# Side steps ordered with a slack behind their modelled ready time, and output-gate columns one head later, in a one-core hybrid decoder step

## The chip, the cores and the metric

The kernel runs on one core of one Trainium2 chip. The metric is the device time of one execution in microseconds (us), the median of several runs. The engines are TensorE (PE; its weight loads are listed apart as PEld), VectorE (DVE), ScalarE (ACT), GpSimd (POOL) and SyncE (SP), which here issues the DMAs. Each engine works through its own instructions strictly in the order in which the program lists them, and waits on semaphores for the operands that other engines make.

## The reference, cut to what matters

One layer is computed for 1024 prompt tokens and for 64 sample tokens (8 sequences of 8) with the same weights:

```python
proj = einsum("bld,de->ble", x, w_in)
glu_a, glu_b, conv_gate, qkv, dn_gate, beta_in, decay_in, mem_q, mem_gate = split(proj)
u = glu_a * sigmoid(glu_b);  hc, _ = causal_dwconv(u, conv_prev, conv_w)          # width 31
out_conv = silu(layer_norm(hc + conv_b)) * silu(conv_gate)
q, k, v = split(silu(causal_dwconv(qkv, qkv_prev, qkv_conv_w)))                    # width 4
o, s = gated_delta_rule(l2norm(q), l2norm(k), v, g, beta, s0)                       # 8 heads of 128
out_dn = rmsnorm(o) * delta_norm_w * silu(dn_gate)
out_mem = softmax(mem_q @ mem_k.T) @ mem_v * silu(mem_gate)                         # 4 heads, 256 memory tokens
y = layer_norm(alpha * x + concat(out_conv, out_dn, out_mem) @ w_out)
```

All data are float32. The gated delta rule is done in chunks of 128 tokens: for each head a triangular matrix is inverted, and then a chain of four chunks carries a 128x128 state. The states are outputs as well.

## The kernel before, in words

**The large products.** The input projection has 52 blocks of 128 output columns. They are computed in two passes, pass one (p = 0) with 512 prompt and the 64 sample tokens, pass two (p = 1) with the other 512 prompt tokens. `gemm` (one call per block) accumulates 16 slices of the contraction in PSUM, in four quarters of four slices. Every product is made of three matmuls on operands split into a high and a low float32r part (`mm3`): ACT casts the weights (`wh`), DVE or POOL makes the rest (`wl`), in `split_quarter`. In pass one a quarter holds two groups of 12 matmuls on 288 columns; in pass two it holds 12 matmuls on 512 columns. Two products for the memory keys and values (`run_mem`) stand ahead of block 44 of pass one. After both passes comes the output projection (PSUM tiles `om`) with the final LayerNorm.

**The side work.** What follows a block is done beside the later blocks. `finish` takes a finished block out of PSUM and adds Python generators to a list, `side.q`: `gen_conv4` (short convolution), `gen_k` (norm, decay matrices, the triangular inverse), `gen_q`, `gen_v`, `gen_s` (the sample tokens), `gen_chain` (the four chunks, the norm, the output gate), for the other groups `gen_cgroup` and `gen_cln` (wide convolution and its LayerNorm) and `gen_att` (memory attention). A generator issues the instructions of one step, and then yields the tiles that its next step reads. A matmul of a later step thus lands in TensorE's single stream between the matmuls of the large products, and TensorE stands still if its operand isn't there yet.

**The order, and the rough clock.** `Side.tick` decides which steps go in. It is called twice a quarter (in pass one after each group of 12 matmuls, in pass two after six matmuls and again after six more). It goes through the list and takes the next step of each generator whose yielded tiles are "ready" by a rough clock, up to six steps and 1000 ns of TensorE work. The clock is the class `Model`: each engine has a time, each tile a ready time; `Proxy` adds for each instruction a cost by formula while the program is being written. For n elements a partition: float32r matmul n/2.4 + 3 ns, float32 matmul max(n/0.6, 110), transpose 109 (n over 64), DVE 65 + n/0.96, ACT 100 + 0.83 n, POOL 100 + 2 n (tensor-tensor); a tile is ready 170 ns after its instruction ends. A generator that yields nothing goes on at the next tick; one that yields "R" may be continued up to three times a tick without a look at the clock (the 31 x 2 small DVE steps of the inverse, the 31 taps of the wide convolution); "B" means blocked on a Python condition. Nothing of this runs on the chip: the clock fixes the order of the instructions when the program is built.

**The order of the blocks.** `ct_order` lists them. Before, each of the eight heads has K, Q, V and its output gate (`COL_DGATE`), then come the GLU pairs, the convolution gates, the memory queries and the memory gates. So head h has its K block at place 4h. The gate block ends in ACT writing a tile `sgate`, from the pool "W" of 19 buffers that all wide side tiles share; it is read by the last multiplication of `gen_chain` (tile `m`), whose result goes to DRAM (`mx`, and `mxs` for the sample tokens) in `put_mixed`.

**Where the order forces a wait.** When the K block of a new head is finished, `finish` calls `side.drain` if three heads are in flight (`inflight`). A drain calls `tick` again and again, with no matmul of the large products in between, and moves the rough TensorE clock on by 200 ns where nothing was taken, until the oldest head has issued its `mx` DMA. `run_mem` and the start of the output projection drain too, until PSUM banks are free, and `open_out` (12 slices into the output projection) drains until no side work is left.

Nearly every instruction bears line 86 in the profile, that of the helper that records it, so groups are told apart by their tiles.

Of the kernel before, what the change touches and what calls it, by code (L numbers as in the profile page):

```python
# [18 lines left out]
NH = 8  # L19
# [2 lines left out]
LN_EPS = 1e-5  # L22
NORM_EPS = 1e-6
HOLD = 10
NSPLIT = 4 * 2 * 52 + 32 + 9 * KT
QSCALE = 128 ** -0.5
NTOK = (576, 512)
# [3 lines left out]
COL_Q, COL_K, COL_V, COL_DGATE = 12, 20, 28, 36  # L31
COL_MQ, COL_MGATE = 44, 48

def ct_order():
    order = []
    for h in range(NH):
        order += [COL_K + h, COL_Q + h, COL_V + h, COL_DGATE + h]
    for j in range(4):
        order += [COL_GLU_A + j, COL_GLU_B + j]
    order += [COL_CGATE + j for j in range(4)]  # L40
    order += [COL_MQ + j for j in range(4)]
    order += [COL_MGATE + j for j in range(4)]
    return order
# [73 lines left out]
class Side:  # L117
# [7 lines left out]
    def tick(self, budget=1000, n=6, rounds=3):  # L125
        m = self.m
        done = 0
        t0 = m.clk["PE"]
        for rnd in range(rounds):
            for e in list(self.q):  # L130
                if done >= n or m.clk["PE"] - t0 >= budget:
                    return done
                if rnd and e[1] != "R":
                    continue
                if e[1] != "R" and m.ready(e[1]) > m.clk["PE"]:
                    continue
                try:
                    r = next(e[0])
                except StopIteration:
                    self.q.remove(e)  # L140
                    done += 1
                    continue
                if r == "B":
                    e[1] = ()
                    continue
                e[1] = r if isinstance(r, tuple) or r == "R" else ()
                if r != "R":
                    done += 1
        return done
# [12 lines left out]
def hybrid_step(ctx, tc, I, O):  # L162
# [21 lines left out]
    def nm(s):  # L184
        uid[0] += 1
        return f"{s}{uid[0]}"
# [36 lines left out]
    written = set()  # L223

    order = ct_order()
    def wsrc(ap):
        f = ap.rearrange("p k c -> p (k c)")
# [61 lines left out]
    def split_quarter():  # L289
# [6 lines left out]
        nsplit[0] += 1  # L296
        wpool, tg = (Y["p"], "y") if nsplit[0] > NSPLIT - (HOLD - 4) else (wp, "")
        hi = wpool.tile([P, 512], F32R, tag="wh" + tg, bufs=4 if wpool is wp else HOLD - 4, name=nm("wh"))
        lo = wpool.tile([P, 512], F32R, tag="wl" + tg, bufs=4 if wpool is wp else HOLD - 4, name=nm("wl"))
        act.copy(out=hi, in_=s)  # L300
# [9 lines left out]
    def ensure(n):  # L310
        while len(ready) < n:
            if not split_quarter():
                return
# [1201 lines left out]
    for g in range(2):  # L1515
# [5 lines left out]
        for cb, idx in phases:  # L1521
# [8 lines left out]
            def out3(i, k, wh, wl):  # L1530
                b, (o, rows) = bank[i], tiles[i]
                if rows == 64:
                    pe.matmul(out=b, lhsT=xfull[k][:, 512:640], rhs=wh, start=(k == 0), stop=False)
                    pe.matmul(out=b, lhsT=xfull[k][:, 512:640], rhs=wl, start=False, stop=(k == KT - 1))
                    return
                sl = slice(o, o + rows)
                pe.matmul(out=b, lhsT=xh[k][:, sl], rhs=wh, start=(k == 0), stop=False)
                pe.matmul(out=b, lhsT=xl[k][:, sl], rhs=wh, start=False, stop=False)
                pe.matmul(out=b, lhsT=xh[k][:, sl], rhs=wl, start=False, stop=(k == KT - 1))

            for k in range(KT - HOLD if last else KT):
                ensure(1)
# [10 lines left out]
            if last:  # L1553
                held = []
                for k in range(KT - HOLD, KT):
                    ensure(1)
# [4 lines left out]
                side.drain(lambda: side.q)  # L1561
                for k in range(KT - HOLD, KT):
                    out3(3, k, *held[k - KT + HOLD])
# [92 lines left out]
```

## Time and profile before

| | us |
|---|---|
| Median of 3 runs (lowest, highest) | 2072.53 (2071.78, 2075.76) |
| The profiled execution's own time | 2066.65 |
| Span of its trace, first to last instruction | 2064.9 |
| PE busy | 1979.0 |
| PEld busy | 1715.8 |
| DVE busy | 1428.7 |
| ACT busy | 845.9 |
| POOL busy | 602.6 |

The profiled execution is 5.88 us shorter than the median. Its mean granted TensorE clock was 0.989 of full speed. In the lists of the profile a group is named by the tiles it writes and reads (`ps<-rbuf,Y`: a side matmul that reads `rbuf` and `Y` and writes a PSUM tile `ps`; `m<-xh,wl`: one of the input projection). "Idle before" is the time in which the engine stood still ahead of an instruction, with the instruction of another engine that ended the wait. The ends of matmuls are modelled, and successive matmuls overlap in the list: what TensorE needs for one is read from start to start. Times in the trace are counted from the first instruction. Pass one lasts until about 905 us (with the memory products near 717 to 760), pass two until about 1640 us, the output projection until the end.

### The profile page before, as it was taken

Reading aid. Unit: us, or ns where it says so; the run is one execution under the profiler, and the core shown is the slowest. Engines: PE = TensorE matmul, PEld = TensorE weight load, DVE = VectorE, ACT = ScalarE, POOL = GpSimd, SP = SyncE. Lnnn points to the kernel's source line nnn. Section 1 sums busy time; section 2 is a strip of 40 time slices with the busy share of each in tenths; the row PEclk is TensorE's granted clock in tenths of the full one; section 3 lists DMA queues with packets and bytes.
Section 4 is the critical chain, followed back from the end, with each engine's and each line's share of the span. In section 5 each row is a group of like instructions: output and inputs, shape, how many; then the busy total and the mean of one; then the engine's idle time right before and its main releaser. Section 6 shows DMA issues by size and latency. Waiting matters only on the chain.

```text
span 2064.9 us, 33208 instructions
## 1 busy us (share of the span) xinstructions
PE 1979.0 (96%) x12156; PEld 1715.8 (83%) x12156; DVE 1428.7 (69%) x3190; ACT 845.9 (41%) x2013; POOL 602.6 (29%) x680
## 2 busy tenths in 40 slices
PE   8999999999999989989999999999989999999995
PEld 7999999999999969977777887787767788877784
DVE  6778877887789984245787776779985433348447
ACT  5444444444433335364444444443326522235124
POOL 5434333443323342113333333322322100006003
PEclk9999999999999999999999999999999999999998
DMA  6232233323223255354332223332232463345444
GB/s 205 84 107 83 97 97 102 93 81 105 90 88 107 96 168 171 108 176 149 96 92 90 74 89 103 102 92 82 90 101 92 153 203 106 106 160 181 142 131 144
DMA packets 107267, 239.50 MB, mean 116 GB/s; under 512 B 32224, under 2 KB 36576, under 8 KB 106848
## 3 DMA queue, kind: packets, MB, share of 16 engines
q1 hardware_dynamic: 107104, 237.39, 36.3%
q8 instruction: 95, 1.56, 0.3%
q14 instruction: 68, 0.56, 0.1%
HBM read 210.24 MB, written 27.10 MB: 115 GB/s over the span
## 4 chain that ended last, share of the span: by engine, by line
PE 36%; DVE 13%; issue 2%; ACT 2%; POOL 1%; DMA 1%; SPq 0%; POOLq 0%; DVEq 0%; ACTq 0%
PE om L86 17%; PE m L86 16%; PE ps L86 4%; DVE hc L86 4%; DVE cv L86 2%; DVE wl L86 2%; DVE y L86 1%; DVE xt L86 1%; DVE X L86 1%; DMA raw<-mx 0%; ACT wh L86 0%; ACT L86 0%; POOL wl L86 0%; POOL y L86 0%; DMA mvs<-out_mem_v_dram 0%
## 5 line engine op out<-in xcount | busy, mean ns | idle before, releaser
L86 PE MATMUL m<-xh,wh 128*128 128x288 f32 (+1 forms) x2496 | 859.4, 344 | 3.6 <-ACT wh L86 3.5
L86 PE MATMUL m<-xh,wl 128*128 128x288 f32 (+1 forms) x2496 | 819.8, 328 | 12.3 <-DVE wl L86 9.6
L86 PE MATMUL m<-xl,wh 128*128 128x288 f32 (+1 forms) x2496 | 816.4, 327 | 0.0
L86 ACT CAST wh<-raw 128x512 fp32r<-128x512 f32 x592 | 359.5, 619 | 398.9 <-PE om L86 221.4
L86 POOL TENSOR_TENSOR wl<-raw,wh 128x512 fp32r<-128x512 f32 x221 | 307.3, 1391 | 728.1 <-ACT wh L86 687.1
L86 PEld LDWEIGHTS m<-xh,wl 128*128 128x128 f32 x2496 | 469.3, 188 | 54.3 <-DVE wl L86 15.1
L86 PEld LDWEIGHTS m<-xh,wh 128*128 128x128 f32 x2496 | 470.5, 188 | 47.0 <-issue 11.1
L86 PEld LDWEIGHTS m<-xl,wh 128*128 128x128 f32 x2496 | 470.9, 189 | 30.2 <-issue 2.7
L86 DVE TENSOR_TENSOR wl<-raw,wh 128x512 fp32r<-128x512 f32 x371 | 283.2, 769 | 264.7 <-ACT wh L86 264.1
L86 DVE SCALAR_TENSOR_TENSOR hc<-u,cvc,hc 128x512 f32<-128x512 f32 x360 | 243.8, 721 | 3.1
L86 PE MATMUL om<-wl,xh 128*128 128x512 f32 x576 | 227.8, 395 | 10.3 <-DVE wl L86 9.2
L86 PE MATMUL om<-wh,xh 128*128 128x512 f32 x576 | 227.4, 395 | 3.9 <-ACT wh L86 2.7
L86 PE MATMUL om<-wh,xl 128*128 128x512 f32 x512 | 201.7, 394 | 0.0
L86 DVE TENSOR_TENSOR xt<-mb,X 128x8 f32<-128x8 f32 (+30 forms) x496 | 183.0, 369 | 11.8
L86 DVE SCALAR_TENSOR_TENSOR cv<-xr,qcw,cv 128x512 f32<-128x512 f32 (+1 forms) x216 | 167.1, 774 | 7.7
L86 POOL TENSOR_TENSOR y<-y,lnb 128x512 f32<-128x512 f32 (+1 forms) x32 | 51.7, 1639 | 342.6 <-DVE y L86 222.9
L86 PEld LDWEIGHTS om<-wl,xh 128*128 128x128 f32 x576 | 109.6, 190 | 37.8 <-DVE wl L86 13.7
L86 PEld LDWEIGHTS om<-wh,xh 128*128 128x128 f32 x576 | 109.5, 190 | 28.8 <-ACT wh L86 3.8
L86 ACT ACT_TABLE_LOAD x89 | 114.2, 1283 | 44.4 <-DVE smz L86 25.7
L86 DVE TENSOR_REDUCE X<-xt 128x4 f32<-128x8 f32 (+30 forms) x496 | 110.2, 222 | 10.6
L86 PEld LDWEIGHTS om<-wh,xl 128*128 128x128 f32 x512 | 97.4, 190 | 20.3
L86 ACT ACTIVATE oi<-ps,GT 128x128 f32<-128x128 f32 x56 | 20.6, 368 | 207.4 <-DVE r L86 192.8
(307 smaller groups left out, 2032.0 us busy)
## 6 DMA issues: line engine op xcount, KB each, us to landing
raw<-in_wt_dram SPq DMA_DIRECT2D x208, 512.0 KB, 3.8
raw<-in_wo_dram SPq DMA_DIRECT2D x72, 512.0 KB, 3.9
mb<-ysc SPq DMA_DIRECT2D x128, 64.0 KB, 2.2
raw<-mx SPq DMA_DIRECT2D x16, 512.0 KB, 3.9
xt<-in_xp_dram SPq DMA_DIRECT2D x32, 256.0 KB, 4.4
out_y_p_dram<-y SPq DMA_DIRECT2D x32, 256.0 KB, 2.8
raw<-in_xa_dram SPq DMA_DIRECT2D x16, 288.0 KB, 3.9
S<-in_sdelta_dram SPq DMA_DIRECT2D x16, 256.0 KB, 4.7
```

The source lines that it names most:

```text
L86: r = fn(**kw)
```

## The change

A step that waits for tiles is taken only when the rough TensorE clock has passed the ready time of its tiles by 800 ns or more; steps that yield nothing, "R" or "B" are treated as before. The blocks get a new order: K0 Q0 V0, K1 Q1 V1 gate0, K2 Q2 V2 gate1, ..., K7 Q7 V7 gate6, gate7, then as before. So K of head h (h from 1) stands at place 4h - 1, one place earlier than before, and its gate at place 4h + 6 instead of 4h + 3 (head 7: 31 both times).

```diff
+SLACK = 800
...
     for h in range(NH):
-        order += [COL_K + h, COL_Q + h, COL_V + h, COL_DGATE + h]
+        order += [COL_K + h, COL_Q + h, COL_V + h] + ([COL_DGATE + h - 1] if h else [])
+    order += [COL_DGATE + NH - 1]
...
-                if e[1] != "R" and m.ready(e[1]) > m.clk["PE"]:
+                if e[1] != "R" and e[1] and m.ready(e[1]) + SLACK > m.clk["PE"]:
                     continue
```

## The prediction

> **What bounds the kernel now.** The page comes first: its span and the busy time of the engines.
>
> ```profile
> span 2064.9 us, 33208 instructions
> PE 1979.0 (96%) x12156; PEld 1715.8 (83%) x12156; DVE 1428.7 (69%) x3190; ACT 845.9 (41%) x2013; POOL 602.6 (29%) x680
> ```
>
> TensorE carries the time, and the change takes no matmul away. It can gain only where TensorE stands still: 2064.9 - 1979.0 = 86 us, and a little more inside what counts as busy. The second view is the list of waits on TensorE, longest in total first (us, times, longest).
>
> ```profile
> PE mm L86 <- DVE wl L86: 9.8, 4, 4.2
> PE m L86 <- DVE wl L86: 9.6, 13, 1.7
> PE om L86 <- DVE wl L86: 9.2, 6, 5.3
> PE ps L86 <- DVE rbuf L86: 5.6, 9, 1.2
> ...
> PE ps L86 <- DVE S L86: 3.3, 3, 2.2
> ...
> PE ps L86 <- ACT oms L86: 2.5, 1, 2.5
> PE ps L86 <- DVE ut L86: 2.4, 5, 0.5
> PE ps L86 <- ACT cv L86: 2.2, 2, 1.4
> PE ps L86 <- DVE pt L86: 1.4, 3, 0.9
> ...
> PE ps L86 <- POOL lsum L86: 1.2, 1, 1.2
> PE ps L86 <- DVE cq L86: 0.9, 2, 0.7
> PE ps L86 <- DVE r L86: 0.8, 2, 0.5
> ...
> PE ps L86 <- ACT GT L86: 0.6, 1, 0.6
> PE ps L86 <- DVE Rc L86: 0.5, 1, 0.5
> ```
>
> The first three rows are waits for weights; the change doesn't touch how these are split. The eleven `ps` rows are side matmuls whose operand came late: 21.4 us in 30 waits. This is what a later place in the order can remove. The third view, the timeline of one such wait, shows how it comes about (start, duration, instruction).
>
> ```profile
> 399.76 1.27 DVE L86 TENSOR_SCALAR cv<-xr,qcw 128x64 f32<-128x64 f32 x1
> 400.21 0.29 PE L86 MATMUL m<-xl,wh 128*128 128x288 f32 x1
> 400.34 0.29 PE L86 MATMUL m<-xh,wl 128*128 128x288 f32 x1
> 401.07 1.00 DVE L86 SCALAR_TENSOR_TENSOR cv<-xr,qcw,cv 128x64 f32<-128x64 f32 x3
> 401.54 0.29 PE L86 MATMUL m<-xh,wl 128*128 128x288 f32 x1
> 402.10 0.28 DVE L86 COPY rbuf<-ps 32x128 f32<-32x128 f32 x1
> 402.44 0.67 PE L86 MATMUL ps<-rbuf,Y 64*64 64x64 f32 x8 [0.61 <-DVE rbuf L86]
> ```
>
> The four `cv` operations on 64 elements hold VectorE for 1.27 + 1.00 = 2.27 us, while the rough clock counts 4 x (65 + 64/0.96) = 0.53 us. The copy into `rbuf` stands behind them in VectorE's queue, so its tile is late by more than the clock believes, and TensorE waits. The matmuls start 400.34 - 400.21 = 0.13 us apart though each is listed with 0.29: so a listed wait of 0.61 us is really 402.44 - 401.54 - 0.13 = 0.77 us. The 30 waits thus cost about 21.4 + 30 x 0.16 = 26 us.
>
> That addition can be set against the Trainium skill, "Perfetto Trace Analysis", section "Identifying the Most-Contended Engine": matmul busy time says little about the distance to the limit, since the instructions are pipelined, and the busy share of the weight loads says more. By the page's rule the PEld row (83%) would leave room for well over 26 us; the starts in the timeline support the part of it that is added here, and no row says that side operands cause more.
>
> **The change part by part.** *The 800 ns.* For the `rbuf` step the working by the formulas is this. Three copies of 65 + 128/0.96 = 198 ns follow the matmuls before; with 170 ns of hand-over at either end the tiles are ready 934 ns after them. The next tick comes after 12 matmuls, 12 x 123 = 1476 ns by the same clock, so the step went in at the first tick. With the slack it needs 1734 ns and goes in one tick later, 12 x 0.13 = 1.6 us in the trace. That covers 0.77 us. All eleven rows but `S` (longest 2.2) and `oms` (2.5) have a longest wait below one tick, so if every late step moves by a tick some 24 of the 26 us go. But the margin has to stand against a lag of VectorE that the clock doesn't see, here 2.27 - 0.53 = 1.7 us, and steps that were on time may now stand behind such a group. I keep three quarters, 18 us; the bounds are 8 (a third) and 26, plus 2 for waits too short to be listed, 28.
>
> *What the slack costs.* The matmuls themselves are the same, so TensorE pays nothing directly. The cost is that every head takes longer. From the code, the longest path through a head's generators has 28 steps that wait for tiles. The pace at present, in pass two:
>
> ```profile
> 1093.24 0.39 PE L86 MATMUL ps<-S,cv 128*128 128x128 f32 x2
> 1093.67 0.35 DVE L86 SCALAR_TENSOR_TENSOR r<-ps,GT,vs 128x128 f32<-128x128 f32 x1 [0.36 <-PE ps L86]
> 1094.86 0.38 PE L86 MATMUL ps<-r,ubuf 128*128 128x128 f32 x2
> 1095.28 0.35 DVE L86 TENSOR_SCALAR ut<-ps,kz 128x128 f32<-128x128 f32 x1 [0.49 <-PE ps L86]
> 1096.46 0.27 PE L86 MATMUL ps<-ut,kd 128*128 128x128 f32 x1
> ```
>
> One link of the chain takes one tick, 1094.86 - 1093.24 = 1.62 us. By the clock's formulas such a link is ready 170 + 198 + 170 = 538 ns after its matmuls; with the slack 1338 ns, where a tick in pass two is 6 x 216 = 1296 ns plus whatever other side matmuls fall between. So about half of the links move by a tick; in pass one, with 1476 ns, most don't. A growth of 0.8 x 28 = 22 us for a head in pass two is the middle; the bounds are 5 us (the order of VectorE's queue hides most of it) and 28 x 1.62 = 45 us.
>
> Does anyone wait for a head's end? Only the drain at the K block of the fourth head. In the new order that block stands at place 11, where the gate of the third head stood, so the row of that gate gives its time:
>
> ```profile
> 179.72 0.33 SPq L86 DMA_DIRECT2D mx<-m  x1
> 215.37 0.71 ACT L86 ACTIVATE sgate<-m 128x288 f32<-128x288 f32 x2
> 1076.11 0.38 SPq L86 DMA_DIRECT2D mx<-m  x1
> 1081.25 0.60 ACT L86 ACTIVATE sgate<-m 128x512 f32<-128x512 f32 x1
> 1095.05 0.59 ACT L86 COPY xr<-m 128x512 f32<-128x512 f32 x1
> ```
>
> In pass one head 0 is done at 179.7 and the block comes at 215.4, a margin of 36 us: no drain. In pass two head 0 is done at 1076.1. Before, K of head 3 came at 1095.05, 19 us later; now at 1081.25, 5.1 us later. A growth of 22 us makes a drain of 22 - 5 = 17 us, or 17/1.62 = 10 links. In a drain nothing lies between the links, and one takes from the matmul's start to the end of its VectorE operation, 1095.28 + 0.35 - 1094.86 = 0.8 us, and some 0.1 to go on, so 9 us, of which about 3 are side matmuls (0.38 for each link) that have to be done anyway: 6 us of standstill. Later heads start one place (1095.05 - 1081.25 = 14 us) earlier too and so lose no spacing: K to K of the fourth next head stays 12 places, and head 4 onwards gives back at most its present margin. The bounds are 0 (growth below 5) and (45 - 5)/1.62 x 0.9 = 22 us.
>
> *The gate one head later.* The gate of head h comes seven places after its K, so about 7 x 14 = 98 us in pass two; the chain needs it only at its end. Head 0's K comes first in the pass, and the gate's new place 6 lies well ahead of 1076 less the time of place 11 down to 6 (1081.25 - 5 x 14 = 1011), so no chain waits for it. The gate's buffer of pool "W" is held for three places, some 42 us, less in each head; in exchange other tiles live longer by the slack. I put both at nothing: no list of the engines' waits names a W tile waiting for its buffer, and if the cover goes it shows as late weights.
>
> *The heads against the wide convolution.* Two stretches are bound by VectorE, by the windows view (length, PE, PEld, DVE busy):
>
> ```profile
> 647.00:717.00 70.00, 70.00 (x523) 69.56 (x522) 70.00 (x133) 21.49 (x40) 18.12 (x16) 1.00 0.31 102
> 1470.00:1540.00 70.00, 61.49 (x250) 46.26 (x250) 65.10 (x76) 16.62 (x27) 22.31 (x16) 0.98 0.32 99
> ```
>
> Heads 6 and 7 end just ahead of them, start 14 us earlier and take 22 us longer, so 8 us net of their VectorE work could slide in. As TensorE stands still for 8.5 of 70 us in the second, an eighth of 8 us is 1 us; bounds -3 (they end earlier) and +3. The end of pass two is safe: the last side DMA is issued at 1655.07 and the drain in `open_out` lies 12 slices of the output projection, each 14 matmuls of 0.23 us, behind 1640: at about 1679.
>
> ```profile
> 1655.07 0.43 SPq L86 DMA_DIRECT2D mx<-om  x1
> ```
>
> POOL's part of a step moves with it and nothing of the large products waits behind it but the low parts of the weights, split two quarters ahead. On SP the DMAs of the side steps (`mx`, the inverse's transfers, the states) move back with their steps, past weight loads that stood behind them. A load then waits less for a side tile; as five loads are kept ahead, I count nothing, and if that cover goes it is the `wl` rows that grow.
>
> *The sum.* -18 + 6 + 1 = -11 us. The profiled execution's 2066.65 would become 2055.6. The shown median lies 5.9 us above that execution, and a prediction is compared with medians, so 2072.5 - 11 = 2061.5; I give 2061.
>
> **The rivals.** *Slower: the drain eats more than the waits gave.* Place: K of head 3 in pass two (and of heads 4 to 7 if their margins go too). It decides once the growth of a head is over about 5 + 20 = 25 us in links of 1.6 us; at the full 45 us it costs 22, and the gain at its lower end is 8, so +14; middle +6, 2078. For: the margin of 5.1 us is read straight off two rows. Against: in a drain the links take half their usual time, which limits the price. Whether long standstills also slow the clock shows here:
>
> ```profile
> 739.00:745.00 6.00, 5.38 (x13) 4.22 (x14) 6.00 (x14) 0.85 (x2) 0.00 (x0) 0.50 0.82 257
> ```
>
> In the 6 us around the 4.2 us wait for `wl` the granted clock is 0.50. The links of a drain leave gaps of about 0.5 us, so by this row alone I add nothing. The Trainium skill, "TensorE: Matmul & The Clock Gate", section "HAM oscillation — how this bites in real kernels", puts the limit at gaps of about 3.4 us; the row agrees. By that rule a drain that ends in one long wait, for a DMA of the inverse for instance, would run some microseconds at half speed, which speaks against this change.
>
> *No change: the waits only move.* VectorE's unseen lag is 1.7 us in the timeline above, twice the slack, and 26 us of waits is 30 cases among several hundred side steps; a shifted order could meet as many. Then the gain is about 8 and the drain takes 6 to 10 of it: 2071.
>
> *The change doesn't do what it says:* the steps could have been late by the order of the queues alone, so that a step moved back takes its VectorE work back too. For the operand of a step this is not so (it is issued one step earlier), but the chain as a whole keeps its relations. The time would be as in the rival before; I count it there.
>
> **How the numbers follow.** The forecast, faster by the removed waits less one drain, has a chance of 0.66; no change 0.16; slower 0.18. Runs of the kernel before lie within 0.2% (4 us), about what a measurement can tell from no change. The forecast's own range is 2044 (28 us gained, no drain) to 2068. The whole range reaches up to the slower rival's middle: 2044 to 2078. Faster by over 0.2% gets 0.66, within it 0.16, slower 0.18.
>
> **What would show it.** Right: the `rbuf` row of TensorE's waits falls from 5.6 us to below 1, the `ps` rows together from 21.4 to below 8; the weight rows (`wl`) stay within 3 us of theirs; head 0's `mx` DMA in pass two comes some 10 to 20 us later than 1076, and beside it TensorE has a short stretch of many `ps` steps without `m` matmuls. Wrong: `ps` rows of the same total under other names (the waits moved), several such stretches in pass two, or `wl` rows that have grown (buffers or queues of POOL and ACT held up).

## The result and the profile after

The changed kernel takes 2108.02 us (median of 4 runs, 2106.89 to 2110.30), the kernel before 2072.16 on the same chip (4 runs, 2071.35 to 2075.76). The ratio is 1.0171, with a 95% interval of 1.0153 to 1.0189: 36 us slower, where 11 us faster was forecast. The profiled execution of the changed kernel took 2106.89 us. Its page, engines first:

```profile
span 2105.2 us, 33200 instructions
PE 1992.1 (95%) x12156; PEld 1723.8 (82%) x12156; DVE 1440.8 (68%) x3190; ACT 850.5 (40%) x2015; POOL 609.0 (29%) x680
```

The matmuls are the same 12156. The span grew by 40.3 us, 4.4 more than the medians, since the profiled execution of before lies 5.5 us under its median and this one 1.1. TensorE's busy time grew by 13.1, so its idle time by 27. The list of TensorE's waits (total us, times, longest) answers to the one of before:

```profile
PE ps L88 <- DVE S L88: 19.3, 10, 3.3
PE ps L88 <- DVE ut L88: 14.6, 13, 2.8
PE mm L88 <- DVE wl L88: 10.0, 4, 4.2
PE om L88 <- DVE wl L88: 9.1, 4, 5.2
PE m L88 <- DVE wl L88: 8.4, 12, 2.3
...
PE ps L88 <- DVE r L88: 4.1, 5, 1.3
...
PE ps L88 <- ACT cv L88: 3.7, 5, 1.0
PE ps L88 <- DVE X L88: 3.0, 2, 1.8
```

The three weight rows hold what they held (27.5 us against 28.6). The `rbuf` row is gone, as announced. But `S`, `ut` and `r`, the three tiles that the chain of a head makes one after the other, went from 3.3, 2.4 and 0.8 us to 19.3, 14.6 and 4.1. All `ps` rows together are 51.2 us in 43 waits, where before they were 21.4 in 30. That is 29.8 us more.

The timeline of one of the four longest such waits, in pass two, TensorE's and VectorE's rows with GpSimd's:

```profile
1183.39 0.49 DVE L88 TENSOR_SCALAR cv<-xr,qcw 128x512 f32<-128x512 f32 x1
...
1183.89 1.30 POOL L88 TENSOR_TENSOR Dm<-D,triu 128x512 f32<-128x512 f32 x1
1183.92 4.95 DVE L88 SCALAR_TENSOR_TENSOR cv<-xr,qcw,cv 128x512 f32<-128x512 f32 x3
...
1185.27 1.37 POOL L88 TENSOR_TENSOR D<-D,kzn 128x512 f32<-128x512 f32 x1
...
1186.60 1.71 POOL L88 TENSOR_TENSOR wl<-raw,wh 128x512 fp32r<-128x512 f32 x1
...
1187.06 0.39 PE L88 MATMUL m<-xh,wl 128*128 128x512 f32 x1
...
1188.79 0.26 DVE L88 TENSOR_REDUCE X<-xt 128x4 f32<-128x116 f32 x1
...
1189.08 0.36 DVE L88 TENSOR_TENSOR xt<-mb,X 128x120 f32<-128x120 f32 x1
...
1190.39 0.34 DVE L88 SCALAR_TENSOR_TENSOR S<-S,GT,ps 128x128 f32<-128x128 f32 x1
...
1190.78 0.71 PE L88 MATMUL ps<-S,cv 128*128 128x128 f32 x4 [3.34 <-DVE S L88]
```

TensorE takes a matmul every 0.23 us here, so it stands still from 1187.29 to 1190.78, 3.5 us. The operation that it waits for, on the state `S` of one head, takes 0.34 us; it starts at 1190.39 because VectorE works through its queue in order, and ahead of it lie the convolution of the Q block of the head after next (three `cv` operations, 4.95 us together while GpSimd's `Dm` and `D` and then a `wl` run beside them; nearly alone such three take 2.33 us, and there is a row of that at the end) and then five operations of the inverse of the head between the two, 1188.79 to 1190.39. The rough clock counts 3 x (65 + 512/0.96) = 1.8 us and 5 x 0.19 = 0.95 us for these eight, together 2.75; the trace shows 1190.39 - 1183.92 = 6.47. The 3.7 us between come close to the standstill of 3.5. This chain is that of head 2, behind the Q block of head 4. The same wait, 3.3 us in the list, comes again at 1253, 1315 and 1377, in the chains of heads 3, 4 and 5, behind the Q blocks of heads 5, 6 and 7.

A long wait costs more than its length. Three stretches of 4 us from the windows view, each beginning where a wait ended (of 2.19, 2.84 and 3.34 us); the third number from the right is the granted clock:

```profile
528.99:532.99 4.00, 4.00 (x20) 4.00 (x21) 3.83 (x13) 0.87 (x2) 0.25 (x1) 0.58 0.02 4
179.61:183.61 4.00, 4.00 (x31) 4.00 (x32) 3.86 (x13) 0.00 (x0) 0.25 (x2) 1.00 0.34 131
1190.78:1194.78 4.00, 4.00 (x17) 3.53 (x18) 2.18 (x6) 0.87 (x2) 0.80 (x1) 0.63 0.27 78
```

After the 3.34 us wait the clock is 0.63 for 4 us, which is 4 x 0.37 = 1.5 us lost; so the wait is worth about 5 us, and the four of them 20. Over the span the mean granted clock went from 0.989 to 0.984: time lost at a low clock is 2105.2 x 0.016 = 33.7 us, before 2064.9 x 0.011 = 22.7, and so 11 us more. The listed side waits (+29.8) and the clock (+11) make up the 40 us; the lower clock is where most of the 13 us of busy time came from (behind the wait above, matmuls start 1192.64 - 1192.21 = 0.43 us apart, not 0.23). The Trainium skill, "TensorE: Matmul & The Clock Gate", section "HAM oscillation — how this bites in real kernels", puts the limit at idle gaps above about 3.4 us. The trace agrees for the waits of 3.3 us (3.5 from start to start) and differs below: the clock fell after one of 2.19 us, and not after one of 2.84.

Where in the kernel it is lost, by the start of a block's first matmul in the two timelines (us, after less before): pass one +1 at block 8, +5 at 16, +15 at 24, +20 at 32, +20 at 44; pass two +14 at its start, +21 at 16, +32 at 24, +44 at 32, +38 at 48; the output projection begins 40 us later. It grows only while heads are in flight; a little is given back elsewhere.

### The profile page after: what moved, and what is told of

Read it like the earlier page. It is cut to its first block, busy times and chain, and to the rows that moved or that the text cites. A ratio compares the mean times of both kernels' runs of the same rounds, so it can differ in the third digit from the quotient of the medians.

```text
span 2105.2 us, 33200 instructions
## 1 busy us (share of the span) xinstructions
PE 1992.1 (95%) x12156; PEld 1723.8 (82%) x12156; DVE 1440.8 (68%) x3190; ACT 850.5 (40%) x2015; POOL 609.0 (29%) x680
## 3 DMA queue, kind: packets, MB, share of 16 engines
q8 instruction: 95, 1.56, 0.3%
## 5 line engine op out<-in xcount | busy, mean ns | idle before, releaser
L88 DVE TENSOR_TENSOR wl<-raw,wh 128x512 fp32r<-128x512 f32 x371 | 273.4, 743 | 255.9 <-ACT wh L88 248.9
L88 DVE SCALAR_TENSOR_TENSOR cv<-xr,qcw,cv 128x512 f32<-128x512 f32 (+1 forms) x216 | 189.8, 879 | 7.7
L88 PEld LDWEIGHTS om<-wh,xh 128*128 128x128 f32 x576 | 109.9, 191 | 30.6 <-ACT wh L88 5.5
L88 PEld LDWEIGHTS om<-wh,xl 128*128 128x128 f32 x512 | 98.0, 191 | 20.5
```

What stands on the lines that cost most here:

```text
L88: r = fn(**kw)
```

## The experiments

The theory after the result: *the order meets VectorE's backlog*. A step's place is chosen by a clock that doesn't see how late VectorE runs; shifting steps puts chain links behind other work in VectorE's queue, by several us, against which 0.8 us is nothing. The rivals: *longer heads are the cost themselves* (drains, more tiles alive), *the slack on the chain delays the chain*, *the order of blocks does it*, *GpSimd's products beside VectorE do it*. All runs in one table; "side waits" are the `ps` rows of TensorE's waits in the profiled execution, and the clock is its mean granted one. Each ratio is against runs of the kernel before on the same chip.

| run | median us | ratio (95%) | side waits, us in times | clock |
|---|---|---|---|---|
| before (profile) | 2072.5 | 1 | 21.4 in 30 | 0.989 |
| after | 2108.0 | 1.0171 (1.0153 to 1.0189) | 51.2 in 43 | 0.984 |
| e1 order only | 2083.5 | 1.0055 (1.0034 to 1.0075) | 28.1 in 31 | 0.989 |
| e2 slack 300 | 2100.4 | 1.0133 (1.0116 to 1.0151) | 43.8 in 42 | 0.983 |
| e3 products on VectorE | 2094.2 | 1.0101 (1.0085 to 1.0118) | 30.6 in 31 | 0.982 |
| e4 products later | 2105.7 | 1.0157 (1.0142 to 1.0172) | 45.3 in 30 | 0.981 |
| e5 old order, slack 300 | 2095.1 | 1.0113 (1.0097 to 1.0129) | 40.9 in 48 | 0.987 |
| e6 chain 14 ticks later | 2124.9 | 1.0259 (1.0245 to 1.0273) | 57.5 in 36 | 0.979 |
| e7 shift from head 4 on | 2082.6 | 1.0058 (1.0044 to 1.0072) | 30.2 in 42 | 0.989 |
| e8 one inverse step later | 2074.5 | 1.0020 (1.0011 to 1.0028) | 23.8 in 35 | 0.989 |
| e9 chain 7 ticks later | 2118.3 | 1.0230 (1.0215 to 1.0246) | 53.5 in 46 | 0.982 |
| e10 no slack on the chain | 2110.4 | 1.0191 (1.0167 to 1.0214) | 51.6 in 49 | 0.984 |
| e11 slack -300 | 2117.3 | 1.0231 (1.0211 to 1.0251) | 51.1 in 36 | 0.978 |
| e12 before, products on VectorE | 2077.5 | 1.0034 (1.0020 to 1.0049) | 25.4 in 37 | 0.992 |
| e13 after, half the inverse | 2057.2 | 0.9936 (0.9922 to 0.9951) | 17.6 in 21 | 0.989 |
| e14 before, half the inverse | 2055.0 | 0.9933 (0.9913 to 0.9953) | 15.2 in 22 | 0.989 |
| e15 VectorE's cost in the clock | 2093.5 | 1.0112 (1.0097 to 1.0127) | 37.8 in 30 | 0.984 |
| e16 side matmul's cost in the clock | 2070.9 | 1.0002 (0.9993 to 1.0012) | 21.9 in 32 | 0.989 |
| e17 four inverse steps a tick | 2094.9 | 1.0120 (1.0104 to 1.0137) | 34.3 in 42 | 0.989 |
| e18 e16 with slack 200 | 2095.2 | 1.0124 (1.0107 to 1.0141) | 34.6 in 38 | 0.988 |

**The two parts.** The order alone (e1), a smaller slack on it (e2), and the smaller slack on the old order (e5, `SLACK = 300` with the old list of blocks). The slack of 800 on the old order wasn't tried.

```diff
-SLACK = 800
+SLACK = 0        # e1;  300 in e2
```

> The new order of the blocks alone, the slack set to 0 ns. Theory A (the slack lengthens every head, so that its last chunks come into VectorE's queue behind the next-but-one head's Q block, whose convolution is stretched by the GpSimd products Dm and D): the order alone leaves the heads' length as before, 2066 to 2076 us, and TensorE's waits for S and ut stay below 10 us together (before 5.7, after 33.9). Theory B (the earlier K block crowds the side work): most of the loss is here, 2095 us or more, with the S and ut rows near those after the change.

> The changed kernel with a slack of 300 ns instead of 800. Theory A: the heads grow by about three eighths of the growth seen (some 10 us instead of 27 to 33), Dm and D start before or after the Q convolution rather than with it in most heads, and the time is 2070 to 2085 us. Theory B: as after the change, 2100 us or more, since the order is the same.

> The old order of the blocks with a slack of 300 ns. If the slack has a cost of its own, it is the step from the order alone (2083 us) to order and slack of 300 (2100 us): 2085 to 2093 us, TensorE's waits for side operands above those of before by 10 us or more. If the slack only hurts in the new order: 2066 to 2076 us, side waits below those of before.

The order alone costs 11 us, 300 ns on top of it another 17, 800 ns another 8; on the old order 300 ns cost 25. So each part costs by itself, the slack most, and not in proportion to its size. A larger slack doesn't scale a count of late steps: it makes other steps late.

The profiled execution of e1 loses 18 us in the first 16 blocks of pass one and 10 in the first 12 of pass two, and gets some of it back later. At the start of each pass K of head 1 now comes one block sooner behind K of head 0 than before. If that is the cause, it moves with the place of the shift:

```diff
-        order += [COL_K + h, COL_Q + h, COL_V + h] + ([COL_DGATE + h - 1] if h else [])
+        order += [COL_K + h, COL_Q + h, COL_V + h]
+        order += [COL_DGATE + h] if h < 4 else [COL_DGATE + h - 1] if h > 4 else []
```

> The new order without slack, but taken up only from head 4 on: heads 0 to 3 keep their gate block. If the loss of the order alone comes from two heads in a row without a gate block between them, it moves to heads 4 and 5 of each pass and stays 8 to 14 us: 2080 to 2086 us. If it comes from the start of a pass, where nothing else is in flight: 2068 to 2076 us.

In pass one the loss then begins at block 20 (+2 us there, +23 at block 32), and the blocks ahead are as before; in pass two it begins behind block 24 (+19 us there, +26 at block 32, from +17 at the start of the pass). The total is that of e1.

**GpSimd beside VectorE.** `Dm` and `D` go from GpSimd to VectorE, in the changed kernel (e3) and in the one before (e12); or they are left on GpSimd and made two ticks later (e4).

```diff
-        pool.tensor_tensor(out=Dm, in0=D, in1=bc(triu), op=ALU.mult)
+        dve.tensor_tensor(out=Dm, in0=D, in1=bc(triu), op=ALU.mult)
...
-        pool.tensor_tensor(out=D, in0=D, in1=bl(zn, 4, P), op=ALU.mult)
+        dve.tensor_tensor(out=D, in0=D, in1=bl(zn, 4, P), op=ALU.mult)
```

> The changed kernel with the two products Dm and D on VectorE instead of GpSimd (32 operations of 0.7 us more on VectorE). If it is the stretching by GpSimd that makes the chunks late, the Q convolution's group falls from 5.5 to about 2.9 us, the waits of 3.3 us for S in pass two go, and the time is 2085 to 2098 us. If the length of the heads alone does it, S and ut rows stay above 25 us together and the time is 2105 us or more.

> The kernel before with Dm and D on VectorE. If the stretching by GpSimd costs only where the Q convolution meets the products (4 of 16 heads before, 13 after): 2066 to 2076 us, against 14 us gained by the same edit after the change. If the edit is good by itself: 2050 to 2064 us.

> The changed kernel with the step that holds the products Dm and D two ticks later (two more empty yields ahead of it), so that GpSimd begins them when the Q convolution is over. By the stretching: convolution groups of 5.5 us become rare, the waits of 3.3 us for S go, 2085 to 2098 us. By the length of the heads alone: heads some 3 us longer still, no gain, 2105 to 2112 us.

In e3 the two rows of the chain fall back to near those of before:

```profile
PE ps L88 <- DVE ut L88: 4.3, 4, 2.5
PE ps L88 <- DVE S L88: 4.2, 7, 2.1
```

That takes 14 us off the changed kernel, though VectorE has more to do; the same edit adds 7 us to the kernel before (a little more than expected). Of the 16 Q blocks, the four `cv` operations take over 5 us in 12 with the change, in 4 before, and in 3 in e3. So the change has brought the convolutions beside the products, and that is a part of its cost. It isn't needed for a loss, though: in e2, 28 us slower than before, only 2 of the 16 take over 5 us. e4 missed: the convolutions moved along with the products (10 of 16 over 5 us), and the waits went to `ut` (20.5 us) and others.

**Is a longer head the cost?** A head, from the start of the first `cv` of its K block to that of the write of `m`, takes 146 us in pass one and 136 in pass two before (mean of heads 1 to 6), 184 and 165 with the change. e6 and e9 make heads long with no slack at all, by empty ticks ahead of the chain; e10 takes the slack off the chain; e11 was to make heads shorter by a negative slack on the kernel before, e17 by four steps a tick instead of three for the inverse (and for the wide convolution, to which the same limit applies).

```diff
     def gen_chain(u):
...
         gt = u["gt"]
+        for _ in range(14):        # e6;  7 in e9;  both with SLACK = 0
+            yield
```

> The new order without slack, and the chain of every head begun 14 ticks later (14 empty yields, about 20 us, near the growth of a head by the slack). If it is the place of the chain beside the next heads' work that costs, and not what the slack does to a single step: 2095 to 2112 us, S, ut and r rows together above 20 us. If the place is harmless: 2078 to 2088 us as with the order alone.

> The new order without slack, the chain begun 7 ticks later (half of the 14 that cost 41 us). If a later chain costs in proportion: 2098 to 2110 us. If it is a matter of what it meets, it needs not lie between 2083 (none) and 2125 us (14 ticks): then anything from 2080 to 2130 us, with the waits in other rows.

```diff
-                if e[1] != "R" and e[1] and m.ready(e[1]) + SLACK > m.clk["PE"]:
+                if e[1] != "R" and e[1] and m.ready(e[1]) + SLACK * (e[0].__name__ != "gen_chain") > m.clk["PE"]:
```

> The changed kernel with the slack on all generators but gen_chain, whose links go in at the first tick as before. If the chain's own slower pace is what costs, its waits fall and the time is 2083 to 2095 us. If it is that the chain begins later, 2098 to 2110 us, S, ut and r rows above 20 us together.

```diff
-                if e[1] != "R" and m.ready(e[1]) > m.clk["PE"]:
+                if e[1] != "R" and e[1] and m.ready(e[1]) + (-300) > m.clk["PE"]:
```

> The kernel before with steps taken 300 ns ahead of their modelled ready time, the opposite of the change. If shorter heads are what helps: heads 5 to 10 us shorter, 2055 to 2069 us. If early steps meet operands that are not there yet: side waits above 35 us, 2076 to 2095 us.

```diff
-    def tick(self, budget=1000, n=6, rounds=3):
+    def tick(self, budget=1000, n=6, rounds=4):
```

> The kernel before with up to four operations of the inverse in a tick instead of three. If VectorE's backlog decides: side waits above 30 us although the heads are 5 to 10 us shorter, 2080 to 2115 us. If long heads were the trouble: 2055 to 2069 us.

With longer heads the kernel is 55 and 48 us slower than before (e6, e9), of which 11 are the order's; but shorter ones cost too: 26 us with 139 and 124 us a head (e17), lost while heads are in flight. e11, 47 us slower, doesn't tell the two apart: of its 52 us of span 46 are lost in pass one, where its heads came out longer (176 us), and some 7 in pass two, where they are shorter (122). Its waits are on other links of the same kind:

```profile
PE ps L86 <- DVE ut L86: 25.1, 12, 3.0
PE ps L86 <- DVE Rc L86: 9.8, 5, 2.0
```

So a loss comes with shorter heads (e17) as with longer ones, and the slack on the chain doesn't matter (e10: nothing changes). And 14 ticks cost hardly more than 7, some 42 and 36 us over e1, where a cost by length would have doubled. Whether length by itself does harm, a run further down shows.

**One step by itself.** The `rbuf` step of the prediction's own example, moved one tick later in every head of the kernel before:

```diff
         yield (U, R)
+        yield
         ps = yield from getps()
```

> The kernel before with one empty yield ahead of the one step that reads rbuf, 1.6 us later in pass one. If a late operand is cured by moving its own step: the rbuf row falls from 5.6 to below 1.5 us and the time is 2063 to 2069 us. If the waits only move: other ps rows grow by as much, 2070 to 2076 us.

```profile
PE ps L86 <- DVE ut L86: 9.4, 13, 1.3
PE ps L86 <- DVE S L86: 5.7, 7, 0.9
PE ps L86 <- DVE Rc L86: 3.8, 5, 0.8
```

The row of `rbuf`, 5.6 us, is gone, and `ut`, `S` and `Rc` have grown by 7.0, 2.4 and 3.3 us. All side waits together grew by 2.4 us, and the kernel is 4 us slower. One step of each head, moved by a single tick, shows the change in small.

**The backlog at a fixed order.** The deciding pair. In every second column of the inverse the two VectorE operations are left out, while the rough clock still counts them: each engine gets its other instructions in the very same order (the traces have the same sequence on every engine but for the 480 operations left out), and VectorE has some 145 us less to do. The inverse is then incomplete.

```diff
+            if i % 2 == 0:
+                c = 65 + 4 * (i + 1) / 0.96
+                md.run("DVE", c, [tmp], [mb, X])
+                yield "R"
+                md.run("DVE", c, [X], [tmp])
+                yield "R"
+                continue
```

> The changed kernel with the VectorE operations of every second column of the triangular inverse left out (the inverse is incomplete), the rough clock still counting them, so that the order on every engine stays the same. If VectorE's backlog makes the side operands late: TensorE's side waits fall from 51 to below 28 us and the time by 20 to 35 us, to 2073 to 2088 us. If the steps depend on each other too closely in this order: waits stay above 42 us, the time above 2098 us.

> The kernel before with the same operations left out and the same order. Control: little to gain, since side waits are 21 us already. With a backlog as the cause 2058 to 2070 us; if the operations left out cost time by themselves, in any order, it falls by as much as in the kernel after, to 2050 us or less.

Against the kernel before on their own chips, the changed kernel is 35.9 us above, e13 13.2 below and e14 15.4 below. So the same operations are worth 49 us in the changed order and 15 in the old one. Without them the two orders differ by 2.2 us instead of 36, and the intervals of the two ratios lie over each other. Both fell further than expected. In e14 the side waits fell by 6.2 us and the span by 15.6, so these operations cost something in the old order too that the waits don't show. TensorE's waits in e13, and the same place of the timeline as above:

```profile
PE ps L88 <- DVE S L88: 6.7, 8, 1.0
PE ps L88 <- DVE ut L88: 3.1, 4, 1.4
```

```profile
1155.35 4.96 DVE L88 SCALAR_TENSOR_TENSOR cv<-xr,qcw,cv 128x512 f32<-128x512 f32 x3
...
1159.79 0.39 PE L88 MATMUL m<-xh,wl 128*128 128x512 f32 x1
...
1160.23 0.34 DVE L88 TENSOR_TENSOR xt<-mb,X 128x120 f32<-128x120 f32 x1
...
1160.61 0.28 DVE L88 TENSOR_REDUCE X<-xt 128x4 f32<-128x120 f32 x1
1160.80 0.34 DVE L88 SCALAR_TENSOR_TENSOR S<-S,GT,ps 128x128 f32<-128x128 f32 x1
...
1161.19 0.71 PE L88 MATMUL ps<-S,cv 128*128 128x128 f32 x4 [1.01 <-DVE S L88]
```

The stretched convolution is there as before (4.96 us; 11 of 16 Q blocks over 5 us), but `S` comes behind it with two operations of the inverse between, not five, and the wait is 1.01 us, not 3.34. The heads are still long, 176 and 152 us, and count as many blocks as in the changed kernel (10.4 and 10.7, against 10.5 and 10.7): length alone does no harm. This shows the cause of the 36 us: VectorE's backlog, which in the changed order lies ahead of links of the chain (`S`, `ut` and `r` fell from 38.0 to 10.6 us). That it is more work than the rough clock counts is read from the timelines.

**A truer clock.** If the clock's errors are the cause, a better clock should mend the order. e15 raises VectorE's fixed cost towards the trace's (0.28 us and 0.36 for operations of 120 elements that the formula puts at 0.19). e16 halves the cost of a side matmul: eight `ps` matmuls on 128 columns take 0.81 us from the first start to that of the next matmul, 0.10 each, where the clock counts 0.21. e18 puts a slack of 200 on e16. All have the new order.

```diff
-                c = 65 + n / 0.96 * (8 if op == "reciprocal" else 1)
+                c = 125 + n / 0.96 * (8 if op == "reciprocal" else 1)        # e15
...
-                    c = n / 2.4 + 3 if kw["rhs"].dtype == F32R else max(n / 0.6, 110)
+                    c = n / 2.4 + 3 if kw["rhs"].dtype == F32R else n / 1.2 + 5        # e16, e18
```

> The new order without slack, the rough clock's fixed cost of a VectorE operation 125 ns instead of 65 (the traces show 280 to 290 ns for 128 elements, where the clock has 198). If the error of the clock is the cause: below 2076 us, side waits below 25 us. If any other order costs: 2085 to 2120 us with side waits above 35 us.

> The new order without slack, the rough clock's side matmul n/1.2 + 5 ns instead of max(n/0.6, 110), near what the traces show from start to start. If the error of the clock is the cause: below 2076 us. If any other order costs: 2085 to 2120 us with side waits above 35 us.

> The kernel of e16 with a slack of 200 ns. If a slack helps once the clock is near: side waits below 18 us, 2060 to 2068 us. If it only deals the collisions anew: side waits 22 to 45 us, 2070 to 2095 us.

e15 is 12 us slower than e1 (both against the kernel before on their own chips). e16 takes the 11 us of the order back: 2070.9, the same as before. e18 is 25 us slower than e16 (both against the kernel before), with the waits in yet another row (ScalarE makes this tile out of VectorE's convolution):

```profile
PE ps L88 <- ACT cv L88: 13.4, 10, 3.4
```

Truer numbers don't reliably give a better order. That e16 did may be due to the formula or to chance in where the steps then fell; one order can't say.

In most runs the span follows the waits and the clock. In e6 the waits grew by 36.1 us and the time lost at a low clock by 2124.3 x 0.021 - 22.7 = 21.9, together 58, and the span by 59.4. In e3, e9 and e11 the same sum gives 24, 47 and 54, the spans grew by 27, 52 and 52. In e1, e7, e12, e17 and e18 it falls 7 to 13 us short of the growth of the span, in e14 9 us short of its fall, and what makes up the rest is open. No run with the whole computation beat the kernel before.

## Why the prediction was wrong

**The step that failed** is the first term: "if every late step moves by a tick some 24 of the 26 us go", of which three quarters, 18 us, were kept. It took the 30 waits for 30 late steps in an order that is otherwise on time, and asked what a tick more does to those. For the step of its example that held: the `rbuf` row went. But moving every step changes everywhere which operations stand ahead of which in VectorE's queue, and a link of the chain behind a stretched convolution and five operations of the inverse is 3.7 us late, against a slack of 0.8. Measured: +29.8 us in place of -18. The text had the reason in hand: it read the lag of 1.7 us off its first timeline, wrote that steps on time might now stand behind such a group, and then kept three quarters by judgement, with no row to size it. Its lower bound, a gain of 8, left out a loss altogether.

**The rival "the waits only move"** was right in mechanism and had 0.16. It assumed that as many waits would come back as went, and so a gain left over. The runs show that the old order has few such meetings: of fifteen other orders with the same work on the same engines (all rows of the table but e3, e12, e13 and e14), fourteen have more waits and are 4 to 55 us slower, and one, e16, is equal. Why the old order is so good isn't known from these runs.

**The halved clock** was put at nothing, as gaps in a drain would be 0.5 us. For the waits that came, of 2 to 3.4 us each, it is 11 us of the 40.

**The growth of a head**, 22 us in pass two, was of the right kind and size. By the starts of the blocks a mean head spans 9.5 blocks before and 10.7 after, 1.2 blocks or 17 us at the old pace of 14.1 us a block; the rest of its 29 us is that the blocks themselves take longer. In pass one, where most links were to stay, the reading failed: it grew from 8.7 to 10.5 blocks, 38 us. Which steps moved there isn't shown.

**The drain** of 6 us didn't come. The two rows that decide it:

```profile
1098.42 0.39 SPq L88 DMA_DIRECT2D mx<-m  x1
...
1102.00 0.59 ACT L88 COPY xr<-m 128x512 f32<-128x512 f32 x1
```

Head 0 is done 3.6 us ahead of K of head 3. Both came later by more than 20 us, of which 14 are the later start of the pass; from there head 0's DMA comes 8 us later and K of head 3 some 6. The slower rival, a drain that eats more than the waits gave, thus had the sign and neither the place nor the price.

**Put at little:** the weight rows are within 1.1 us of theirs, so the gate's later place and the queues of SP and GpSimd cost nothing that these rows show. The heads against the wide convolution were put at +1 (-3 to +3); in pass two the lag falls from +44 at block 32 to +38 at block 48, so this stretch gave 6 us back, outside these bounds.

## What to carry to other kernels

In a hand-ordered program an operand is late because of what stands ahead of it in its engine's queue, so a slack has to be set against the measured lag of that queue (here 3.7 us, not 0.8; whether a slack of that size would help, no run shows), and moving all steps makes other steps late instead of curing the late ones alone. Size such a change from both sides of zero; the few long standstills count most, as the clock falls behind them. To find the cause, keep the order of every engine and take work out of the suspected queue: if two orders then take the same time, the backlog was the difference.

## What was not expected of the hardware

A VectorE operation on 512 elements can take far longer while a GpSimd operation runs beside it. Three of these with GpSimd at work only for the first 0.1 and the last 0.2 us, in the kernel before:

```profile
397.51 2.33 DVE L86 SCALAR_TENSOR_TENSOR cv<-xr,qcw,cv 128x512 f32<-128x512 f32 x3
```

The first of the three in the changed kernel's timeline, beside `Dm`:

```profile
1183.92 1.82 DVE L88 SCALAR_TENSOR_TENSOR cv<-xr,qcw,cv 128x512 f32<-128x512 f32 x1
```

So nearly alone one takes 2.33 / 3 = 0.78 us; this one takes 1.04 us more, most of the 1.30 us that `Dm` takes. The Trainium skill, "GPSIMD Engine Reference", section "1. Specifications", says that the SBUF interfaces are shared with VectorE and names contention with operations that have two SBUF inputs; this one has, and the rows agree, with a size that the page doesn't give. Of the 144 such operations on 512 elements in the changed kernel, the 57 with no GpSimd operation beside them all take 0.75 us; the 39 that run for nine tenths or more beside GpSimd's tensor-tensor operations take 0.75 to 1.86, 1.56 in the mean. The mean of all 144 went from 991 ns (142.7 us together) to 1128:

```profile
L86 DVE SCALAR_TENSOR_TENSOR cv<-xr,qcw,cv 128x512 f32<-128x512 f32 x144 | 142.7, 991 | 5.1
L88 DVE SCALAR_TENSOR_TENSOR cv<-xr,qcw,cv 128x512 f32<-128x512 f32 x144 | 162.4, 1128 | 5.1
```

That is 162.4 - 142.7 = 19.7 us more work for VectorE out of no more operations. VectorE's busy time as a whole grew by 12.1 us, as other rows fell.
